# One work list for both layers of a two-layer encoder trunk: adding transfers, row sums and fillers placed elsewhere in the order

## The chip, the cores and the metric

The kernel runs on one core of one Trainium2 chip. The metric is device time in microseconds (us). Times of one kernel are medians of several runs; a profiled execution gives the trace on which the reading rests.

The engines are TensorE (PE, matmuls and transposes; its weight loads are listed as PEld), VectorE (DVE), ScalarE (ACT), GpSimd (POOL) and SyncE (SP). Each runs its own instructions in order, and they meet through semaphores. Transfers between the chip's main memory and the on-chip memory are issued by SP, ACT or POOL, and run on 16 DMA engines.

## The reference

Two layers run over a sequence of 512 rows of width 1024, in float32. Cut to its core, a layer is:

```python
h = x @ w_in[l]                     # 1024 x 9216, cut into eleven parts
o_a = retention(rq, rk, rv, rg)     # 4 heads, chunkwise recurrent form
o_b = chunk_attention(cq, ck, cv)   # 8 heads, relative bias, chunk-causal
o_c = diff_attention(dq, dk, dv)    # 4 heads, difference of two softmaxes
g = sigmoid(gates + b_merge[l])     # three gates per channel
merged = g0 * (o_a @ w_a) + g1 * (o_b @ w_b) + g2 * (o_c @ w_c)
x = layer_norm(ALPHA * x + merged @ w_out)
u_gate, u_up = split(x @ w_ffn_in)  # hidden width 2816
x = layer_norm(ALPHA * x + (silu(u_gate) * u_up) @ w_ffn_out)
```

## The kernel before

**Numbers.** Every float32 operand of a product is carried as a pair, a rounded high part and the rest as a low part, both in the format float32r. One product is three matmuls: high by high, high by low, low by high (`mm3`, lines 166 to 170). The pair is made by one cast on ACT (high) and one subtract on DVE (low). For activations this is `split` with `part_hi` and `part_lo` (lines 152 to 160); for weights it is line 203 and the one after it (plain tiles, class `Wt`, two halves each), and lines 310 and 311 (staged blocks, class `Staged`).

**Seven products in place of eight.** Most large products are done as 2 by 2 blocks by a scheme of Winograd's kind: seven block products, called m1, m2, y, x, g, v and h, on sums and differences of blocks. The sums of weights are made partly by DMA: the first block is loaded on SP (line 223), and a second is added to it on its way by a transfer that POOL issues with an add (line 227, `more`). Such a transfer is called an adding transfer here. Class `Adds` (input projections and FFN input) has two per problem: `a`, used by y, x and h, and `c`, used by g; where x and h need one more block, DVE adds it (line 307). Class `Chain` (FFN output) changes its block `a` in place: y is split, then an adding transfer turns `a` into what x needs, then, after x's split, a second turns it into what h needs (`take`, with `then`). m1, m2 and v are plain loads. The sums of activations are called row sums: for the input x they are made by `Quarters.turned` (lines 337 to 340 and two splits, s12 and s43), one call per pair of row blocks, named q0 to q3 in the list. The hidden rows of the FFN get theirs in class `Hidden` (steps h0.y, h0.m1 and so on; tiles hqh and hql).

**Memory.** Loaded weights lie in 4 buffers (`st`), split weights in 3 pairs of buffers (`wh`, `wl`), activations in 61 buffers of 128 by 512, and results of matmuls in 8 banks of PSUM. A block's load must wait until the split of an earlier block has freed its `st` buffer, and a split until PE has done with the block three before it.

**The order.** It is written out by hand in the string `ORDER` (lines 59 to 99). Entries are parted by `;`. The first word names an item, that is, one weight block and its matmuls: `w` (the values of attention b and c), `R` (queries and keys of the retention), `G1` (a gate), `p` and `q` (values and gates of the retention), `g20` and the like (plain gate tiles), `cqk` and `dqk` (queries and keys of the two attentions), `b01` (branch 0, tile 1), `out`, `ffn`, `i0` to `i3` (FFN input), `f18` to `f21` (plain FFN input tiles), `o0` and `o1` (FFN output) and `rest`. After it, parted by `|`, stand steps that are put between the item's jobs: after the first job, after the second, and so on. `+` splits the next block that isn't split yet (`prepare`). `w.a`, `w.c`, `o1.a` and so on issue the load and the adding transfer. `c1.3` to `c3.3` and `d0.30` to `d4.3` are the steps of the attentions: scores with softmax (c1, d0), transposes (c2, d2), products with the values (c3, d3) and the last transposes (d4). `rr`, `rf`, `rs` and `r1` to `r3` belong to the retention. Before each item, loads are issued until three blocks are ahead, and the item's own block is split if it is not yet (`run_items`).

The list gives each instruction its turn; the framework then lays out each engine's queue and may let an instruction of a later entry go ahead where it finds the engine free. In the string of before, the two layers have a list each, parted by `@`.

Of the kernel before, what the change touches and what calls it, by code (L numbers as in the profile page):

```python
# [55 lines left out]
NATURAL = ("m1", "m2", "y", "g")  # L56


ORDER = """first | q1 w.a ; w.m1 | + | + q2 q0 q3 ; w.m2 | lam | + w.c ; g03 ; w.y | + ; w.x |  | + ;
w.g | + + | R.a + ; w.v ; w.h | R.c + + | + ; R.m1 ; R.m2 |  | + ; R.y |  | + ; R.x | rr.000 | + ;  # L60
R.g | rr.010 | G1.a + ; R.v | + rr.101 ; R.h | rr.111 | G1.c ; G1.m1 | + rr.100 ; G1.m2 |  | + rr.110 ;
G1.y | rr.001 ; G1.x | rr.011 ; G1.g | + | rf.0 ; G1.v | dh.0 rs.0 | + ; p.m1 | p.a | r1.0 ;
G1.h | dh.1 | + ; p.m2 | p.c rf.1 | rs.1 + ; p.y |  | + ; p.x |  | + ; p.g | r1.1 q.a | + ; p.v |  | + ;
q.m1 | + | + ; p.h |  | r2.0 ; q.m2 | q.c + rf.2 r2.1 | + dh.2 ; q.y ; q.x | rs.2 | r3.1 ;
q.g | r3.0 rf.3 | + rs.3 dh.3 + ; q.v | r1.2 ; q.h | + r1.3 ; cqk1 | + + r2.3 r2.2 | r3.3 ; cqk0 | r3.2 ;
b01 | c1.0 | c1.1 vbc c2.0 + ; b02 | c1.2 + c3.0 c2.1 | c1.3 ; cqk2 |  | c3.1 c2.2 + + ;
b00 | c1.4 c3.2 | c2.3 c1.5 ; cqk3 | c3.3 + | c2.4 ; b03 | c1.6 + c3.4 c1.7 vbd + | c2.5 + ;
dqk0 | c3.5 c2.6 c2.7 | c3.6 ; dqk1 |  | d0.00 c3.7 ; b10 ; g20 | d0.01 + d0.10 | d2.0 ;
b13 | d3.0 + | + d0.11 ; dqk2 |  | + d2.1 ; b11 |  | d0.20 + d3.1 ; dqk3 | d0.21 d4.0 ; b12 | + | d2.2 + ;
g21 | + d0.30 | d3.2 d0.31 ; g23 | + | d2.3 ; g22 | d4.1 d4.2 d3.3 | + d4.3 ; b20 | + + ; b21 ; b22 |  | + ;  # L70
out0 ; b23 | + | + ; out1 ; out2 ; ffn | i0.a | i0.c + ; i0.m1 | n1 + | + n0 ; i0.m2 | + + ;
i0.y | + | + n2 ; i0.x ; i0.g |  | + i1.a n3 + ; i0.h ; i0.v ; i1.m1 | i1.c | + ; i1.m2 |  | + ; i1.y | + + ;
i1.x ; i1.g | i2.a | + ; i1.h |  | + + ; i1.v |  | + ; i2.m1 | i2.c + ; i2.m2 | + | + ; i2.y | + | + ; i2.x ;
i2.g |  | i3.a + ; i2.h |  | + ; i2.v | + ; i3.m1 ; i3.m2 | i3.c ; i3.y | + ; i3.x |  | + ;
i3.g |  | o0.a + ; i3.h |  | + o0.c o0.begin h0.y + ; i3.v |  | + ; f18 | + h0.m1 o0.rows ;
o0.m1 | h0.m2 | h0.x ; o0.y | + | h0.g ; o0.m2 | + + | h0.v ; f19 ; o0.x | h0.h | o1.begin + o1.a ;
o0.v |  | h1.y ; o0.g | + + | + ; o0.h | h1.m1 + o1.c | + ; o1.y | + h1.x + | h1.m2 ; o1.m1 ; o1.m2 ;
f20 | h1.v | + ; o1.x | h1.g h1.h + ; o1.g | + | + ; o1.v |  | + + ; f21 ; o1.h | + ; rest0 ; rest1 | + | + ;
rest2 ; @ ; first | + w.a q1 ; w.m1 |  | lam + q2 q0 q3 ; w.m2 |  | + ; g03 | w.c ; w.y | + ; w.x |  | + ;
w.g | + + | R.a + ; w.v ; w.h | R.c + + | + ; R.m1 ; R.m2 |  | + ; R.y |  | + ; R.x | rr.000 | + ;  # L80
R.g | rr.010 | G1.a + ; R.v | + rr.101 ; R.h | rr.111 | G1.c ; G1.m1 | + rr.100 ; G1.m2 |  | + rr.110 ;
G1.y | rr.001 ; G1.x | rr.011 ; G1.g | + | rf.0 ; G1.v | dh.0 rs.0 | + ; p.m1 | p.a | r1.0 ;
G1.h | dh.1 | + ; p.m2 | p.c rf.1 | rs.1 ; p.y |  | + + ; p.x |  | + ; p.g | r1.1 | + ; p.v | q.a | + ;
q.m1 | + | + ; p.h |  | r2.0 ; q.m2 | q.c + rf.2 r2.1 | + dh.2 ; q.y ; q.x | rs.2 | r3.1 r3.0 ;
q.g |  | rf.3 + + ; q.v | rs.3 dh.3 | r1.2 ; q.h | + | r1.3 + ; cqk1 | + r2.3 r2.2 | r3.3 ; cqk0 | r3.2 ;
b01 | c1.0 | c1.1 vbc c2.0 + ; b02 | c1.2 + c3.0 c2.1 | c1.3 ; cqk2 |  | c3.1 c2.2 + + ;
b00 | c1.4 c3.2 | c2.3 c1.5 ; cqk3 | c3.3 + | c2.4 ; b03 | c1.6 + c3.4 c1.7 vbd + | c2.5 ;
dqk0 | + c3.5 c2.6 c2.7 | c3.6 ; dqk1 |  | d0.00 c3.7 ; b10 ; g20 | d0.01 + d0.10 | d2.0 ;
b13 | d3.0 + | + d0.11 ; dqk2 |  | d2.1 + ; b11 |  | d0.20 + d3.1 ; dqk3 | d0.21 d4.0 ; b12 |  | d2.2 + ;
g21 | + d0.30 + | d3.2 d0.31 ; g23 | + | d2.3 ; g22 | d4.1 d4.2 d3.3 | + d4.3 ; b20 | + + ; b21 ;  # L90
b22 |  | + ; out0 ; b23 |  | + ; out1 | + ; out2 ; ffn | i0.a | i0.c + ; i0.m1 | n1 + | + n0 + ; i0.m2 | + ;
i0.y | + | + ; i0.x ; i0.g | n2 | + i1.a n3 + ; i0.h ; i0.v ; i1.m1 | i1.c | + ; i1.m2 |  | + ; i1.y | + + ;
i1.x ; i1.g | i2.a | + ; i1.h |  | + + ; i1.v |  | + ; i2.m1 | i2.c + ; i2.m2 | + | + ; i2.y | + | + ; i2.x ;
i2.g |  | i3.a + ; i2.h |  | + ; i2.v | + ; i3.m1 ; i3.m2 | i3.c | + ; i3.y ; i3.x |  | + ;
i3.g |  | o0.a + ; i3.h |  | + o0.c o0.begin h0.y + ; i3.v |  | + ; f18 | + h0.m1 o0.rows ;
o0.m1 | h0.m2 | h0.x ; o0.y | + | h0.g ; o0.m2 | + + | h0.v ; f19 ; o0.x | h0.h | o1.begin + o1.a ;
o0.v |  | h1.y ; o0.g | + + | + ; o0.h | h1.m1 + o1.c | + ; o1.y | + h1.x + | h1.m2 ; o1.m1 ; o1.m2 ;
f20 | h1.v | + ; o1.x | h1.g h1.h + ; o1.g | + | + ; o1.v |  | + + ; f21 ; o1.h | + ; rest0 ; rest1 | + | + ;
rest2"""


# [1 line left out]
def trunk(ctx, tc, x_in, xT_in, w_in, ret_norm_g, da_norm_g, lq1, lk1, lq2, lk2, w_a, w_b, w_c, b_merge, w_out,  # L103
# [463 lines left out]
    def item(specs, fn, *groups):  # L567

        items.append((specs, fn, groups))
# [75 lines left out]
    def layer(l):  # L645
# [933 lines left out]
        for i, it in enumerate(fout_rest(0) + fout_rest(1)):  # L1579
            its[f"rest{i}"] = it  # L1580
        fns["+"] = prepare
        for line in ORDER.split("@")[l].strip("; \n").split(";"):
            name, *groups = [part.split() for part in line.split("|")]
            item(*its[name[0]], *[[fns[n] for n in grp] for grp in groups])

# [8 lines left out]
    for l in range(LAYERS):  # L1594
        layer(l)
# [48 lines left out]
```

## Time and profile before

| | us |
|---|---|
| median of 3 runs | 1905.19 |
| lowest and highest run | 1901.96, 1908.35 |
| the profiled execution | 1906.96 |
| its span, from the first to the last instruction | 1905.2 |
| PE busy in the span | 1872.0 |
| DVE busy | 1393.9 |
| ACT busy | 1024.5 |
| mean granted clock of PE, as a share of full speed | 0.994 |

How to read it: a row of a timeline has the start, the duration, the engine, the line of the kernel, the operation, the output and the inputs, and in brackets how long the engine had been idle before, and who released it. A row of the waits has the waiting engine with its tile and line, whom it waited for, the total, the times and the longest. The granted clock is the share of TensorE's full clock in a stretch; at half of it a matmul takes about twice as long. Matmuls are pipelined, so the start-to-start distance of two of them is shorter than the duration of one.

### The profile page before, as it was taken

What the parts mean: (1) busy time and instruction counts of PE and PEld (TensorE: products, weight loads), DVE (VectorE), ACT (ScalarE), POOL (GpSimd) and SP (SyncE); (2) the same over time, 40 slices, a digit from 0 to 9 for tenths busy, and PEclk for the clock granted to TensorE, in tenths of its full rate; (3) what the DMA queues carried; (4) which work ended last, traced back from release to release, by engine and by line L of the source; (5) the groups of instructions that cost most, each with busy time, mean ns of one, the idle gap of its engine ahead of it and who ended that gap; (6) DMA issues with size and microseconds to landing.
All of it is one profiled execution on the core that took longest, in us unless ns stands there. A gap on an engine that the chain in (4) does not pass through costs nothing. (4 is left out here: it accounts for less than half of the span.)

```text
span 1905.2 us, 27735 instructions
## 1 busy us (share of the span) xinstructions
PE 1872.0 (98%) x10930; PEld 1655.2 (87%) x10930; DVE 1393.9 (73%) x2029; ACT 1024.5 (54%) x1651; POOL 116.8 (6%) x125
## 2 busy tenths in 40 slices
PE   9899999999999999999999999999999999999998
PEld 7799888887888999987898998888788889999876
DVE  4777876668757977786577878766686679777766
ACT  4556666677643644453265565576766345445431
POOL 0000100000001000010000001000000010000100
PEclk9999999999999999999999999999999999999999
DMA  8797755243256396876467896453332655769841
GB/s 278 219 271 228 194 177 160 67 149 111 78 171 188 96 241 164 234 190 165 144 191 232 230 255 193 149 172 101 109 118 94 204 133 160 183 180 252 208 134 45
DMA packets 233207, 327.29 MB, mean 172 GB/s; under 512 B 10751, under 2 KB 109173, under 8 KB 233077
## 3 DMA queue, kind: packets, MB, share of 16 engines
q1 hardware_dynamic: 197812, 260.50, 41.4%
q0 software_dynamic: 27456, 54.53, 16.4%
q10 hardware_dynamic: 7808, 10.49, 1.5%
q8 instruction: 86, 1.41, 0.3%
q14 instruction: 45, 0.36, 0.1%
HBM read 293.97 MB, written 31.51 MB: 171 GB/s over the span
## 5 line engine op out<-in xcount | busy, mean ns | idle before, releaser
L168 PE MATMUL pt<-xTh,wh 128*128 128x256 f32 (+1 forms) x1392 | 460.8, 332 | 0.9 <-ACT wh L203 0.9
L169 PE MATMUL pt<-xTl,wh 128*128 128x256 f32 (+1 forms) x1392 | 458.2, 329 | 1.3 <-DVE xTl L158 1.3
L170 PE MATMUL pt<-xTh,wl 128*128 128x256 f32 (+1 forms) x1392 | 458.1, 329 | 0.0
L311 DVE TENSOR_TENSOR wl<-st,wh 128x2048 fp32r<-128x2048 f32 x154 | 352.1, 2288 | 141.0 <-ACT wh L310 140.7
L310 ACT CAST wh<-st 128x2048 fp32r<-128x2048 f32 x154 | 293.5, 1910 | 277.6 <-PE pt L169 125.5
L169 PEld LDWEIGHTS pt<-xTl,wh 128*128 128x128 f32 x1392 | 265.6, 191 | 24.0 <-DVE xTl L158 1.8
L170 PEld LDWEIGHTS pt<-xTh,wl 128*128 128x128 f32 x1392 | 265.2, 191 | 23.8
L168 PEld LDWEIGHTS pt<-xTh,wh 128*128 128x128 f32 x1392 | 264.9, 191 | 23.9 <-ACT wh L203 1.6
L204 DVE TENSOR_TENSOR wl<-st,wh 128x1024 fp32r<-128x1024 f32 (+1 forms) x172 | 181.6, 1071 | 103.8 <-ACT wh L203 101.1
L203 ACT CAST wh<-st 128x1024 fp32r<-128x1024 f32 (+1 forms) x172 | 155.4, 928 | 168.5 <-issue 74.5
L168 PE MATMUL pt<-s43h,wh 128*128 128x256 f32 x384 | 109.1, 284 | 0.0
L169 PE MATMUL pt<-s12l,wh 128*128 128x256 f32 x384 | 108.9, 284 | 0.0
L170 PE MATMUL pt<-s12h,wl 128*128 128x256 f32 x384 | 108.9, 284 | 0.0
L168 PE MATMUL pt<-s12h,wh 128*128 128x256 f32 x384 | 108.9, 283 | 0.0
L169 PE MATMUL pt<-s43l,wh 128*128 128x256 f32 x384 | 108.8, 283 | 0.0
L170 PE MATMUL pt<-s43h,wl 128*128 128x256 f32 x384 | 108.8, 283 | 0.0
L168 PE MATMUL pf<-wh,hqh 128*128 128x512 f32 x224 | 89.9, 402 | 4.3 <-ACT hqh L154 4.3
L170 PE MATMUL pf<-wh,hql 128*128 128x512 f32 x224 | 90.0, 402 | 1.6 <-DVE hql L160 1.6
L169 PE MATMUL pf<-wl,hqh 128*128 128x512 f32 x224 | 89.2, 398 | 0.0
L307 DVE TENSOR_TENSOR st<-st 128x2048 f32<-128x2048 f32 x36 | 82.3, 2285 | 0.7 <-DMA st<-in_w_in 0.3
L168 PEld LDWEIGHTS pt<-s43h,wh 128*128 128x128 f32 x384 | 73.8, 192 | 0.2
L168 PEld LDWEIGHTS pt<-s12h,wh 128*128 128x128 f32 x384 | 73.8, 192 | 0.0
(306 smaller groups left out, 4008.5 us busy)
## 6 DMA issues: line engine op xcount, KB each, us to landing
st<-in_w_in SPq DMA_DIRECT2D x64, 1024.0 KB
st<-in_w_ffn_in SPq DMA_DIRECT2D x40, 1024.0 KB
st<-in_w_ffn_out SPq DMA_DIRECT2D x24, 1024.0 KB
st<-in_w_in POOLq DMA_DIRECT2D x20, 1024.0 KB, 10.1
st<-in_w_in SPq DMA_DIRECT2D x32, 512.0 KB
st<-in_w_ffn_in POOLq DMA_DIRECT2D x16, 1024.0 KB, 10.0
st<-in_w_ffn_out POOLq DMA_DIRECT2D x16, 1024.0 KB, 10.2
st<-in_w_ffn_in SPq DMA_DIRECT2D x24, 512.0 KB
```

The costliest lines, as they stand in the source:

```text
L168: nc.tensor.matmul(ps, lh, rh, start=start, stop=False, skip_group_check=more)
L169: nc.tensor.matmul(ps, lh, rl, start=False, stop=False, skip_group_check=more)
L170: nc.tensor.matmul(ps, ll, rh, start=False, stop=stop, skip_group_check=more)
L203: return [nc.scalar.copy(self.hi[:, a:b], self.st[:, a:b]), nc.vector.tensor_sub(self.lo[:, a:b], self.st[:, a:b], f(self.hi[:, a:b]))]
L204: nc.vector.tensor_sub(self.lo[:, a:b], self.st[:, a:b], f(self.hi[:, a:b]))]
L307: nc.vector.tensor_add(st, st, ap)
L310: nc.scalar.copy(self.hi, st)
L311: nc.vector.tensor_sub(self.lo, st, f(self.hi))
```

## The change

`ORDER` is replaced by one list that both layers use; the function that reads it takes the whole string for each layer instead of the part before or after `@`. The items, their matmuls, loads, splits and steps are the same; only their places differ.

In the first items of each layer (before, layer 0, then after):

```diff
-first | q1 w.a ; w.m1 | + | + q2 q0 q3 ; w.m2 | lam | + w.c ; g03 ; w.y | + ; w.x |  | + ;
+first | q1 + w.a | + q2 ; w.m1 |  | lam + q0 q3 ; w.m2 ; g03 | w.c + ; w.y |  | + ; w.x |  | + ;
```

Layer 1 had `first | + w.a q1 ; w.m1 |  | lam + q2 q0 q3 ; w.m2 |  | + ; g03 | w.c ; w.y | + ; w.x |  | + ;`.

In the attentions (before is layer 0; in layer 1 some `+` stood elsewhere):

```diff
-b01 | c1.0 | c1.1 vbc c2.0 + ; b02 | c1.2 + c3.0 c2.1 | c1.3 ; cqk2 |  | c3.1 c2.2 + + ;
+b02 | c1.0 | c1.1 vbc c2.0 + ; b01 | c1.2 + c3.0 c2.1 | c1.3 ; cqk2 |  | c3.1 c2.2 + ;
...
-dqk0 | c3.5 c2.6 c2.7 | c3.6 ; dqk1 |  | d0.00 c3.7 ; b10 ; g20 | d0.01 + d0.10 | d2.0 ;
-b13 | d3.0 + | + d0.11 ; dqk2 |  | + d2.1 ; b11 |  | d0.20 + d3.1 ; dqk3 | d0.21 d4.0 ; b12 | + | d2.2 + ;
-g21 | + d0.30 | d3.2 d0.31 ; g23 | + | d2.3 ; g22 | d4.1 d4.2 d3.3 | + d4.3 ; b20 | + + ; b21 ; b22 |  | + ;
+dqk0 | + c2.6 c2.7 c3.5 | c3.6 ; dqk1 |  | d0.00 c3.7 ; b10 ; g20 | d0.01 + + d0.10 | d2.0 ;
+b13 | d0.11 | d3.0 ; dqk2 | d2.1 + ; b12 | d3.1 | d0.20 + ; dqk3 | + d4.0 | d0.21 ; b11 | + | + ;
+g21 | d2.2 + | d0.30 d3.2 d0.31 ; g23 | + + | d2.3 ; g22 | d4.1 d4.2 d3.3 | d4.3 ; b20 | + ; b21 ;
```

In the FFN output (both layers):

```diff
-i3.g |  | o0.a + ; i3.h |  | + o0.c o0.begin h0.y + ; i3.v |  | + ; f18 | + h0.m1 o0.rows ;
-o0.m1 | h0.m2 | h0.x ; o0.y | + | h0.g ; o0.m2 | + + | h0.v ; f19 ; o0.x | h0.h | o1.begin + o1.a ;
-o0.v |  | h1.y ; o0.g | + + | + ; o0.h | h1.m1 + o1.c | + ; o1.y | + h1.x + | h1.m2 ; o1.m1 ; o1.m2 ;
-f20 | h1.v | + ; o1.x | h1.g h1.h + ; o1.g | + | + ; o1.v |  | + + ; f21 ; o1.h | + ; rest0 ; rest1 | + | + ;
+i3.g |  | o0.begin o0.a + ; i3.h |  | + o0.c o0.rows h0.y ; i3.v |  | h0.m1 + ; f18 ; o0.m1 |  | + ;
+o0.y | + | h0.x h0.m2 ; o0.m2 | h0.v | + + ; f19 | h0.h h0.g | + ; o0.x |  | o1.begin o1.a ; o0.g | + + ;
+o0.v | + | h1.y ; o0.h | h1.m1 + | + o1.c ; o1.m1 | + + | h1.m2 ; o1.y | h1.x ; o1.m2 |  | + ;
+f20 | h1.v | + ; o1.x | h1.h | h1.g ; o1.v | + + ; o1.g ; f21 |  | + ; o1.h | + ; rest0 ; rest1 | + + ;
```

Elsewhere the `+` stand at other places too; two more pairs of items change sides (`R.h` goes behind `G1.m1`, `i2.v` ahead of `i2.h`), some steps of the retention move by a job or two, and `p.a`, `q.a`, `q.c` and `i2.a` move by up to an item. The function:

```diff
-        for line in ORDER.split("@")[l].strip("; \n").split(";"):
+        for line in ORDER.split(";"):
```

More of the change, by code (lines that the diff above doesn't have):

```diff
@@ L56 @@
 NATURAL = ("m1", "m2", "y", "g")
[L59 to L63, printed above, removed]
@@ L64 @@
-q.m1 | + | + ; p.h |  | r2.0 ; q.m2 | q.c + rf.2 r2.1 | + dh.2 ; q.y ; q.x | rs.2 | r3.1 ;
-q.g | r3.0 rf.3 | + rs.3 dh.3 + ; q.v | r1.2 ; q.h | + r1.3 ; cqk1 | + + r2.3 r2.2 | r3.3 ; cqk0 | r3.2 ;
-b01 | c1.0 | c1.1 vbc c2.0 + ; b02 | c1.2 + c3.0 c2.1 | c1.3 ; cqk2 |  | c3.1 c2.2 + + ;
-b00 | c1.4 c3.2 | c2.3 c1.5 ; cqk3 | c3.3 + | c2.4 ; b03 | c1.6 + c3.4 c1.7 vbd + | c2.5 + ;
-dqk0 | c3.5 c2.6 c2.7 | c3.6 ; dqk1 |  | d0.00 c3.7 ; b10 ; g20 | d0.01 + d0.10 | d2.0 ;
-b13 | d3.0 + | + d0.11 ; dqk2 |  | + d2.1 ; b11 |  | d0.20 + d3.1 ; dqk3 | d0.21 d4.0 ; b12 | + | d2.2 + ;
@@ L70 @@
-g21 | + d0.30 | d3.2 d0.31 ; g23 | + | d2.3 ; g22 | d4.1 d4.2 d3.3 | + d4.3 ; b20 | + + ; b21 ; b22 |  | + ;
[L71 to L74, printed above, removed]
@@ L75 @@
-i3.g |  | o0.a + ; i3.h |  | + o0.c o0.begin h0.y + ; i3.v |  | + ; f18 | + h0.m1 o0.rows ;
-o0.m1 | h0.m2 | h0.x ; o0.y | + | h0.g ; o0.m2 | + + | h0.v ; f19 ; o0.x | h0.h | o1.begin + o1.a ;
-o0.v |  | h1.y ; o0.g | + + | + ; o0.h | h1.m1 + o1.c | + ; o1.y | + h1.x + | h1.m2 ; o1.m1 ; o1.m2 ;
-f20 | h1.v | + ; o1.x | h1.g h1.h + ; o1.g | + | + ; o1.v |  | + + ; f21 ; o1.h | + ; rest0 ; rest1 | + | + ;
-rest2 ; @ ; first | + w.a q1 ; w.m1 |  | lam + q2 q0 q3 ; w.m2 |  | + ; g03 | w.c ; w.y | + ; w.x |  | + ;
@@ L80 @@
[L80 to L95, printed above, removed]
@@ L96 @@
-o0.m1 | h0.m2 | h0.x ; o0.y | + | h0.g ; o0.m2 | + + | h0.v ; f19 ; o0.x | h0.h | o1.begin + o1.a ;
-o0.v |  | h1.y ; o0.g | + + | + ; o0.h | h1.m1 + o1.c | + ; o1.y | + h1.x + | h1.m2 ; o1.m1 ; o1.m2 ;
-f20 | h1.v | + ; o1.x | h1.g h1.h + ; o1.g | + | + ; o1.v |  | + + ; f21 ; o1.h | + ; rest0 ; rest1 | + | + ;
+ORDER = """first | q1 + w.a | + q2 ; w.m1 |  | lam + q0 q3 ; w.m2 ; g03 | w.c + ; w.y |  | + ; w.x |  | + ;
+w.g | R.a + | + + + ; w.v ; w.h | R.c + ; R.m1 | + + ; R.m2 | + ; R.y | + + ; R.x | rr.000 ;
@@ new lines @@
+R.g | rr.101 rr.010 | G1.a + ; R.v | + ; G1.m1 | + rr.100 ; R.h | rr.111 | G1.c ; G1.m2 |  | rr.110 ;
+G1.y | + | + rr.001 ; G1.x | rr.011 ; G1.g |  | + rf.0 ; G1.v | dh.0 rs.0 ; p.m1 |  | p.a r1.0 ;
+G1.h | dh.1 + | + ; p.m2 | p.c | rf.1 ; p.y ; p.x | + rs.1 | + ; p.g | + | r1.1 q.a ; p.v |  | + ;
+q.m1 | + | rf.2 ; p.h | + | r2.1 q.c ; q.m2 |  | + r2.0 + dh.2 ; q.y ; q.x | rs.2 | r3.1 r3.0 ;
+q.g | rf.3 | + rs.3 + dh.3 + ; q.v | r1.2 ; q.h | r1.3 | + ; cqk1 | + + r2.3 r2.2 | r3.3 ; cqk0 | r3.2 ;
@@ new lines @@
+b02 | c1.0 | c1.1 vbc c2.0 + ; b01 | c1.2 + c3.0 c2.1 | c1.3 ; cqk2 |  | c3.1 c2.2 + ;
+b00 | c1.4 c3.2 | c2.3 c1.5 ; cqk3 | c3.3 + | c2.4 + ; b03 | c1.6 + c3.4 c1.7 vbd | c2.5 ;
+dqk0 | + c2.6 c2.7 c3.5 | c3.6 ; dqk1 |  | d0.00 c3.7 ; b10 ; g20 | d0.01 + + d0.10 | d2.0 ;
+b13 | d0.11 | d3.0 ; dqk2 | d2.1 + ; b12 | d3.1 | d0.20 + ; dqk3 | + d4.0 | d0.21 ; b11 | + | + ;
+g21 | d2.2 + | d0.30 d3.2 d0.31 ; g23 | + + | d2.3 ; g22 | d4.1 d4.2 d3.3 | d4.3 ; b20 | + ; b21 ;
+b22 |  | + ; out0 ; b23 |  | + ; out1 ; out2 | + ; ffn | i0.a | + ; i0.m1 | n1 + | n0 ; i0.m2 | + i0.c + ;
@@ new lines @@
+i0.y | + | + n2 ; i0.x ; i0.g |  | + i1.a n3 + ; i0.h ; i0.v ; i1.m1 | i1.c | + ; i1.m2 |  | + + ; i1.y ;
+i1.x | + ; i1.g |  | + ; i1.h | i2.a | + + ; i1.v |  | + ; i2.m1 | i2.c + ; i2.m2 | + + | + ; i2.y | + ;
+i2.x ; i2.g |  | i3.a + ; i2.v ; i2.h | + ; i3.m1 ; i3.m2 | i3.c | + ; i3.y ; i3.x |  | + ;
+i3.g |  | o0.begin o0.a + ; i3.h |  | + o0.c o0.rows h0.y ; i3.v |  | h0.m1 + ; f18 ; o0.m1 |  | + ;
+o0.y | + | h0.x h0.m2 ; o0.m2 | h0.v | + + ; f19 | h0.h h0.g | + ; o0.x |  | o1.begin o1.a ; o0.g | + + ;
```

## The prediction

> **What bounds the kernel now.** I read the page's first part, then the waits of TensorE (PE), then stage windows around each wait, then each engine's timeline there.
>
> ```profile
> span 1905.2 us, 27735 instructions
> PE 1872.0 (98%) x10930; PEld 1655.2 (87%) x10930; DVE 1393.9 (73%) x2029; ACT 1024.5 (54%) x1651; POOL 116.8 (6%) x125
> ```
>
> PE is the bound: 33.2 us of the span are not busy. The change leaves every matmul in place, so it can win only what PE loses in waits, and what the clock loses around them. The waits of PE (total, times, longest):
>
> ```profile
> PE pf L168 <- ACT hqh L154: 4.3, 2, 2.3
> PE psc L442 <- ACT ks L152: 4.2, 2, 2.1
> PE pf L170 <- DVE s12l L158: 3.3, 2, 2.1
> PE pt L168 <- ACT obh L152: 3.0, 2, 1.5
> PE pf L168 <- ACT s12h L152: 2.1, 1, 2.1
> PE pf L170 <- DVE hql L160: 1.6, 2, 0.8
> PE psc L442 <- ACT th L1147: 1.1, 2, 0.5
> ```
>
> "2 times" is mostly once per layer. Three places hold most of it: the FFN output (hqh, hql), the row sums of x (s12, layer 0 only) and late attention (ks). The windows around them (PE, weight load, DVE, ACT, POOL busy, then granted clock, DMA share, GB/s), the FFN output and late attention in both layers:
>
> ```profile
> 63.00:79.00 16.00, 10.62 (x38) 7.61 (x37) 13.61 (x21) 7.54 (x11) 1.28 (x1) 0.89 0.45 159
> 471.00:476.00 5.00, 2.92 (x13) 2.28 (x12) 4.35 (x7) 4.18 (x6) 0.00 (x0) 0.85 0.24 87
> 866.00:878.00 12.00, 9.14 (x27) 6.74 (x26) 9.36 (x11) 5.58 (x6) 1.28 (x1) 0.72 0.53 167
> 1414.00:1419.00 5.00, 2.89 (x15) 2.19 (x14) 4.36 (x6) 3.83 (x6) 0.00 (x0) 1.00 0.38 139
> 1808.00:1820.00 12.00, 8.96 (x26) 6.52 (x25) 9.36 (x11) 5.58 (x6) 1.28 (x1) 0.72 0.50 156
> ```
>
> The loss at a place is its idle time plus (1 - clock) x window. FFN output: 4.3 + 1.6 idle, plus 12 x 0.28 = 3.4 in each layer, 12.7 together. Row sums: 3.3 + 2.1 = 5.4 idle, plus 16 x 0.11 = 1.8, so 7.2. Late attention: 4.2 idle, plus 5 x 0.15 = 0.8, so 5.0. **24.9 us in all.**
>
> **Part 1, the FFN output.** Each weight block is split by one ACT cast and one DVE subtract, whose groups on the page are
>
> ```profile
> L311 DVE TENSOR_TENSOR wl<-st,wh 128x2048 fp32r<-128x2048 f32 x154 | 352.1, 2288 | 141.0 <-ACT wh L310 140.7
> L310 ACT CAST wh<-st 128x2048 fp32r<-128x2048 f32 x154 | 293.5, 1910 | 277.6 <-PE pt L169 125.5
> ```
>
> Timelines of PE, ACT, DVE, SP and POOL in layer 0, and the adding transfers' line of the page:
>
> ```profile
> 866.12 0.39 PE L168 MATMUL pf<-wh,hqh 128*128 128x512 f32 x1
> 867.25 0.39 PE L170 MATMUL pf<-wh,hql 128*128 128x512 f32 x1
> 869.71 0.50 PE L168 MATMUL pf<-wh,hqh 128*128 128x512 f32 x1 [2.07 <-ACT hqh L154]
> 867.14 1.99 ACT L203 CAST wh<-st 128x1024 fp32r<-128x1024 f32 x2 [8.16 <-DMA st<-in_w_ffn_in]
> 869.03 0.62 ACT L154 ACTIVATE hqh<-fth 128x512 fp32r<-128x512 f32 x1
> 851.96 2.29 DVE L311 TENSOR_TENSOR wl<-st,wh 128x2048 fp32r<-128x2048 f32 x1
> 854.27 1.97 SPq L196 DMA_DIRECT2D st<-in_w_ffn_in  x2
> 849.25 1.28 POOL L227 DMA_DIRECT2D st<-in_w_ffn_out  x1 [24.48 <-DVE wl L311]
> 850.95 1.28 POOL L227 DMA_DIRECT2D st<-in_w_ffn_out  x1 [0.42 <-issue]
> st<-in_w_ffn_out POOLq DMA_DIRECT2D x16, 1024.0 KB, 10.2
> ```
>
> ACT works in order. The casts of the plain tile f20 (L203) stood 8.16 us for its load; behind them stood the second half of h1.m2's cast (hqh), which PE wanted at 867.5 for o1.m2, after six matmuls of it (866.12 to 867.25 are five steps, 0.227 each). The load was issued at 854.27, when the split of o1.m1 (wl, 851.96 + 2.29) freed its st buffer, and took 12.9 us, because two adding transfers of about 10.2 us each had begun at 849.25 (o1.y's, behind y's split) and 850.95 (o1.c's).
>
> The new list puts o1.m1 ahead of o1.y, one item of 24 matmuls (5.4 us of PE) earlier. What moves: m1's split (ACT cast, DVE subtract) starts 5.4 earlier, so SP issues f20's loads near 848.9; y's split and the adding transfer that POOL issues behind it move 5.4 later, to 854.6. f20's load then shares the engines with o1.c's addition alone. If it takes between 6.3 (1.05 MB at the 167 GB/s of the window 866:878) and the old 12.9, it lands between 855 and 861.8; its casts need a wh buffer, which PE frees at the end of o1.m1, one item and six matmuls before 867.5, at 860.7. So ACT waits at most 1.1, and h1.m2's half, 0.62 of cast, is ready by 865. The casts cost nothing then; the cover is PE's item between. The y transfer, now at 854.6 + 10.2 = 865, meets o1.x's cast, which is wanted only after o1.m2's end (871.6) and f20's 48 matmuls (10.9), at 882: hidden. The x, g, v, h order likewise frees o0.c before v; no wait of PE stood there. I take **12.7** (bounds 0 and 12.7).
>
> On the clock there is a rule to weigh: the window's clock is 0.72 after waits of 2.1 and 0.8 us, but 1.00 after a wait of 2.1 at 1415. The Trainium skill, "TensorE: Matmul & The Clock Gate", section "What's actually happening", has the clock halve after an idle window of about 3.4 us; by that no wait here would slow the clock, and only idle time would come back. The trace disagrees at 866, agrees at 1414; I follow the windows, and keep the other as rival D.
>
> **Part 2, row sums of x.**
>
> ```profile
> 63.11 0.39 PE L168 MATMUL pf<-wh,s12h 128*128 128x512 f32 x1
> 74.00 0.50 PE L170 MATMUL pf<-wh,s12l 128*128 128x512 f32 x1 [2.13 <-DVE s12l L158]
> 40.10 0.42 DVE L337 TENSOR_TENSOR sa<-xf 128x256 f32<-128x256 f32 x1
> 50.24 1.23 DVE L204 TENSOR_TENSOR wl<-st,wh 128x1024 fp32r<-128x1024 f32 x1 [9.04 <-ACT wh L203]
> 61.91 2.29 DVE L307 TENSOR_TENSOR st<-st 128x2048 f32<-128x2048 f32 x1 [0.29 <-DMA st<-in_w_in]
> 64.72 2.28 DVE L307 TENSOR_TENSOR st<-st 128x2048 f32<-128x2048 f32 x1
> 73.26 0.68 DVE L158 TENSOR_TENSOR s12l<-sa,s12h 128x512 fp32r<-128x512 f32 x1
> 37.52 0.37 SPq L223 DMA_DIRECT2D st<-in_w_in  x1
> 53.01 20.73 SPq L223 DMA_DIRECT2D st<-in_w_in  x3
> ```
>
> w.y wants the sums q0 to q3 from 63.1 on; the last half came at 73.9. DVE had stood 9.04 us at g03's split, with q1's fourth operation behind it, and between the late sums ran two additions for w.x and w.h (L307, 4.6) and two splits (4.6): 9.2 us of work not yet wanted. The new list puts q1 and q2 ahead of g03's split and q0, q3 right behind it, and w.x's split behind all of w.y. A sum is four quarter operations (0.42) and two differences (0.68), about 3 us of DVE; two of the four now fit the 9.04 us gap, and 9.2 of foreign work lies lower. The last half was wanted nine matmuls into w.y, at 65.1, and came 8.8 late: the second alone covers that, and the first adds 6. That is 7.2 won.
>
> A price goes with it. Buffers of loads are handed out in list order: before, w.c's load took the one freed at 37.5 and w.x's the one at 53.0; now w.x's load is issued first (three blocks ahead, at g03), so w.c's goes out near 53. It landed then in 8.9 (53.01 to 61.9), POOL adds 1.28 and 10.2, ACT's cast 1.9: 75.3, and the subtract 2.3 more. PE reaches w.g at 63.1 + 2 x 5.4 = 73.9: a wait of 1.4 to 3.7, or about nothing if the load takes 6.3. I take 2. Behind that cast stand ACT's copies of w.x's result (tu), which only later sums want. Part 2: **5.2** (bounds -3.7 and 7.2). Layer 1 had no such wait; it loses and gains nothing.
>
> **Part 3, late attention.**
>
> ```profile
> 473.99 0.99 PE L442 MATMUL psc<-ks,qs 128*128 128x512 f32 x4 [2.08 <-ACT ks L152]
> 466.88 1.08 ACT L152 CAST dPh<-ptr 128x512 fp32r<-128x512 f32 x2
> 468.25 2.35 ACT L404 COPY sw<-pt 32x512 f32<-32x512 f32 x4
> 472.68 2.54 ACT L152 CAST ks<-rot 64x512 fp32r<-64x512 f32 x4
> L1109 PE MATMUL pdo<-vhl,dPh 128*128 128x256 f32 x64 | 18.2, 346 | 0.0
> ```
>
> d0.20's scores (psc) wait for dqk2's key: its rotary copies begin behind d2.1's casts (1.1 us). The new list runs d2.1 between dqk2's two projections, so these casts leave the key's path, and d3.1 goes ahead of d0.20: 8 matmuls of this form and 2 like them, 0.346 each when alone, about 0.12 when packed (256 columns, half of 0.227), so 1.2 to 3.5 us of filler. Together 2.3 to 4.6 against 2.08: the wait goes, in both layers. d2.1 itself needs d0.11, which moves ahead of d3.0, so its input is not later. The obh wait (3.0) and the th wait (1.1) keep their neighbours (d0.00, c3.7, then b10; d0.01, d0.10 in g20): no change. I take **5.0** (bounds 0 and 9.1).
>
> **The rest of the list** (both layers now share one; splits mostly listed nearer their use; R.h one place later; loads p.a, w.a behind others; first of layer 1 fetched at rest1's end instead of in o1.h) I cannot read item by item. The cover of these moves is that PE waits nowhere else for long; the obh and th waits, 4.1 us, are the kind that stays over in such a list, and a new order can make as many again. I take -3 (bounds -6 and +4.1).
>
> **Sum:** 12.7 + 5.2 + 5.0 - 3 = 19.9. The profiled execution took 1906.96 in all (span 1905.2), 1.8 above the median of 1905.19. From the one 1887.1, from the other 1885.3: **1886 us**, 1% less.
>
> **Rivals.** **A, the load stays late** (chance 0.13): f20's split is still listed before h1.m2's cast, and the addition of o1.c still meets f20's load. If ACT again stands, part 1 gives nothing: 1886 + 12.7 = 1899. For it: the ACT order; against it: a load 5.4 us earlier with one addition less. **B, a new wait for the old one** (0.12): w.g's wait takes 3.7 and, with the clock, some 2 more, and small waits take 6: 1886 + 7 = 1893. **C, slower** (0.11): the splits. Their place in the list is nearer to use: counting the list, 84 of the 227 splits are listed one item or less ahead, 59 before. A split takes 1.9 + 2.3 = 4.2 against an item of 5.4: 1.2 us of slack, which one sum or rotary ahead of it takes. If the 25 newly late ones lose 2 us each, 50 us go: 1886 + 50 = 1936. It decides from 0.8 us each (20 in all), where the gain is gone. Against it: ACT's casts mostly wait for PE to free a wh buffer (125.5), not for their turn, so the list's place does not set their start. **D, the clock does not come back** (0.05): if the slow stretches of 3.4 + 3.4 + 1.8 + 0.8 = 9.4 are not caused by the waits, 1895. The skill's rule named above would have it so. **The forecast as it stands**: 0.59.
>
> **How the numbers follow.** About 0.3%, 5.7 us, is what a measurement can tell from no change: from 1899.5 to 1910.9 is "same". The forecast, B and D are faster (0.76), A lies on the border and goes mostly to same; C is slower. Faster 0.76, same 0.13, slower 0.11. Range: down to 1877 (all 24.9, and the 4 that the rest may win), up over A to 1904, which leaves out C and little else.
>
> **What would show it.** Right: no PE wait on hqh, s12 or ks; in the FFN output f20's L196 loads before y's L227; windows there at clock 1.00. Wrong: ACT's L203 waiting for st<-in_w_ffn_in near 860; PE waiting at w.g (pf, s43) for wh; new rows "PE <- ACT wh" or "PE <- DVE wl" summing to more than 6; then the splits are the bound.

## The result, and the profile after

| | median, us | lowest to highest | runs |
|---|---|---|---|
| before | 1904.01 | 1901.96 to 1908.35 | 4 |
| after | 1889.19 | 1888.39 to 1890.41 | 4 |

The ratio is 0.992 (95% interval 0.9901 to 0.9939), that is 15 us less. Line numbers of the changed kernel are 20 lower than before: L168 is now L148, L311 is L291, L223 is L203.

The head of the changed kernel's page, and then its waits of PE (who waits for whom: total us, times, longest). Left out are two rows that both kernels share (warm 1.5, xTl 1.3) and those of 0.5 and less:

```profile
span 1887.4 us, 27746 instructions
PE 1864.0 (99%) x10930; PEld 1648.8 (87%) x10930; DVE 1394.0 (74%) x2029; ACT 1022.9 (54%) x1651; POOL 116.3 (6%) x125
```

```profile
PE pf L150 <- DVE s12l L138: 2.7, 2, 1.7
PE pf L148 <- ACT s12h L132: 2.2, 2, 1.1
PE psc L422 <- ACT th L1127: 2.1, 2, 1.1
PE pro L149 <- DVE rvl L138: 1.5, 2, 0.7
PE pt L148 <- ACT obh L132: 1.1, 2, 0.6
PE pt L148 <- DVE do L1096: 0.9, 2, 0.5
```

The rows for hqh, hql and ks are gone. Those for s12 are not: 4.9 us, where before had 5.4. The windows of the changed kernel (PE, weight load, DVE, ACT, POOL busy, then clock, DMA share, GB/s), at the row sums, at late attention, and at the FFN output of both layers:

```profile
61.50:77.50 16.00, 11.17 (x40) 7.85 (x39) 14.50 (x24) 7.62 (x13) 0.83 (x1) 0.89 0.71 176
462.00:478.00 16.00, 15.55 (x81) 13.26 (x80) 10.21 (x19) 12.01 (x27) 0.00 (x0) 1.00 0.25 83
860.00:872.00 12.00, 12.00 (x55) 9.93 (x54) 9.55 (x11) 4.57 (x4) 1.28 (x1) 1.00 0.86 223
1793.00:1805.00 12.00, 12.00 (x55) 9.93 (x54) 9.46 (x12) 5.72 (x5) 1.28 (x1) 1.00 0.82 216
```

The FFN output now runs without a gap at full clock in both layers. At the row sums PE still stands idle, and the clock is still 0.89. Timelines of SP, POOL and ACT in the changed kernel, at the FFN output of layer 0:

```profile
845.60 0.99 SPq L176 DMA_DIRECT2D st<-in_w_ffn_in  x2
845.81 1.28 POOL L207 DMA_DIRECT2D st<-in_w_ffn_out  x1 [22.17 <-DVE wl L291]
851.30 1.28 POOL L207 DMA_DIRECT2D st<-in_w_ffn_out  x1 [4.21 <-DVE wl L291]
857.69 2.00 ACT L183 CAST wh<-st 128x1024 fp32r<-128x1024 f32 x2 [2.52 <-issue]
```

f20's loads go out ahead of the second adding transfer, and its casts no longer wait for them (8.16 us before). At the row sums of layer 0, the timelines of ACT, SP, DVE and POOL in the changed kernel:

```profile
48.63 0.33 ACTq L1140 DMA_DIRECT2D th<-th  x1
49.06 1.05 ACT L183 CAST wh<-st 128x1024 fp32r<-128x1024 f32 x1 [6.22 <-DMA rows<-in_ln_g]
67.40 1.90 ACT L290 CAST wh<-st 128x2048 fp32r<-128x2048 f32 x1 [3.71 <-DMA st<-in_w_in]
69.21 0.61 ACT L132 CAST s12h<-sa 128x512 fp32r<-128x512 f32 x1
39.80 0.27 SPq L651 DMA_DIRECT2D rows<-in_ln_g  x1
50.14 1.23 DVE L184 TENSOR_TENSOR wl<-st,wh 128x1024 fp32r<-128x1024 f32 x1 [7.90 <-ACT wh L183]
58.28 2.28 DVE L287 TENSOR_TENSOR st<-st 128x2048 f32<-128x2048 f32 x1
58.66 1.28 POOL L207 DMA_DIRECT2D st<-in_w_in  x1 [22.09 <-DVE s12l L138]
```

Read backwards: DVE still stands 7.90 us for ACT's cast of g03. ACT stands because the issue of its own store of a gate tile (th) waits 6 us, by the trace for a small load (rows) that SP issued at 39.80. The kernel before had the same stall, in two pieces (5.85 us here, 1.93 just ahead of g03's cast):

```profile
46.54 0.69 ACT L1147 ACTIVATE th<-pt,hb 128x512 f32<-128x512 f32 x1 [5.85 <-DMA rows<-in_b_merge]
```

From 50.14 until the last row sum is ready, near 74, DVE runs without a gap, so whatever stands in its queue ahead of a row sum delays it. Later ACT stands 3.71 us for w.g's block, whose addition POOL issued at 58.66, and the cast of the last row sum (69.21) is behind it. That second stall costs this sum only about 0.5 us, since DVE had made its input (sa) at 68.72 and no sooner.

### The profile page after: what moved, and what is told of

Read it like the earlier page. It is cut to its first block, busy times and chain, and to the rows that moved or that the text cites. A ratio compares the mean times of both kernels' runs of the same rounds, so it can differ in the third digit from the quotient of the medians.

```text
span 1887.4 us, 27746 instructions
## 1 busy us (share of the span) xinstructions
PE 1864.0 (99%) x10930; PEld 1648.8 (87%) x10930; DVE 1394.0 (74%) x2029; ACT 1022.9 (54%) x1651; POOL 116.3 (6%) x125
## 5 line engine op out<-in xcount | busy, mean ns | idle before, releaser
L148 PE MATMUL pt<-xTh,wh 128*128 128x256 f32 (+1 forms) x1392 | 460.0, 331 | 1.2 <-DVE do L1096 0.9
L291 DVE TENSOR_TENSOR wl<-st,wh 128x2048 fp32r<-128x2048 f32 x154 | 352.5, 2290 | 137.5 <-ACT wh L290 134.7
L148 PEld LDWEIGHTS pt<-xTh,wh 128*128 128x128 f32 x1392 | 264.3, 190 | 24.6 <-DVE do L1096 1.2
L148 PE MATMUL pt<-s43h,wh 128*128 128x256 f32 x384 | 109.1, 284 | 0.1
L148 PE MATMUL pt<-s12h,wh 128*128 128x256 f32 x384 | 108.7, 283 | 0.0
L148 PE MATMUL pf<-wh,hqh 128*128 128x512 f32 x224 | 87.3, 390 | 0.0
L287 DVE TENSOR_TENSOR st<-st 128x2048 f32<-128x2048 f32 x36 | 82.3, 2287 | 0.3
L148 PEld LDWEIGHTS pt<-s43h,wh 128*128 128x128 f32 x384 | 73.7, 192 | 0.7 <-DVE tw L838 0.6
L148 PEld LDWEIGHTS pt<-s12h,wh 128*128 128x128 f32 x384 | 73.7, 192 | 0.0
```

The source lines that it names most:

```text
L148: nc.tensor.matmul(ps, lh, rh, start=start, stop=False, skip_group_check=more)
L287: nc.vector.tensor_add(st, st, ap)
L291: nc.vector.tensor_sub(self.lo, st, f(self.hi))
```

## The experiments

All times are compared with the kernel before, run on the same chip beside them (medians 1905.10, 1903.99 and 1904.23 us for the three groups of four). "Split step" is a `+` of the list.

| run | median (lowest to highest), us | ratio (95% interval) |
|---|---|---|
| e1 FFN output alone | 1895.84 (1890.46 to 1898.27) | 0.995 (0.993 to 0.9969) |
| e2 late attention alone | 1898.24 (1894.58 to 1901.40) | 0.9963 (0.995 to 0.9976) |
| e3 row sums alone | 1917.82 (1913.96 to 1922.24) | 1.0069 (1.005 to 1.0089) |
| e4 one exchange alone | 1893.60 (1893.19 to 1897.09) | 0.9945 (0.9927 to 0.9962) |
| e5 after, small loads late | 1889.53 (1883.91 to 1895.43) | 0.9921 (0.9899 to 0.9942) |
| e6 before, small loads late | 1903.60 (1897.80 to 1907.49) | 0.9987 (0.9971 to 1.0002) |
| e7 row sums alone, same lead | 1903.42 (1900.84 to 1905.92) | 0.9997 (0.9987 to 1.0007) |
| e8 after, exchange undone | 1890.15 (1888.21 to 1892.55) | 0.9923 (0.9907 to 0.994) |
| e9 after, w.c earlier | 1896.45 (1893.27 to 1899.75) | 0.9953 (0.9938 to 0.9969) |
| e10 after, small loads late and w.c earlier | 1892.50 (1890.05 to 1900.88) | 0.9945 (0.9925 to 0.9964) |
| e11 after, FFN output of before | 1899.24 (1897.01 to 1901.42) | 0.9974 (0.9963 to 0.9984) |
| e12 after, once more | 1888.60 (1887.26 to 1891.85) | 0.9919 (0.9904 to 0.9935) |

### The parts, each alone in the list of before (e1, e2, e3)

Each takes one of the blocks of the diff as shown and leaves the rest of the two lists: e1 from `i3.g` to `rest1`, e2 from `b13` to `g21`, e3 from `first` to `w.x`.

> The sequence of before with the new order of the FFN output alone, in both layers. If the three parts are independent, as the forecast's sum has it, the new order gives its whole term: 12.7 us, ratio 0.993, the waits for hqh and hql gone and the clock of that stretch 1.00, while the waits for s12h, s12l and ks stand as before (about 11 us and 4 us). Rival: the gain hangs on where the rest of the list has left the engines by then; the waits stay above 4 us per layer and the ratio is over 0.996.

> The sequence of before with the new late attention alone, in both layers. By the forecast's third step: the two waits for ks (2.1 us each, and the clock behind them) go, 5.0 us, ratio 0.997, and the waits for th and obh stay at 1.1 and 3.0. If the order of the other parts had a hand in what the changed kernel shows, new small waits (do 0.9, th 1.0) come here too and the gain is 3 to 4 us, ratio 0.998.

> The sequence of before with the spread row sums alone, in both layers. The forecast's second step gives 5 to 7 us, ratio 0.997, with the waits for s12h and s12l below 1 us. The theory from the changed kernel's trace: ScalarE is held by a store whose issue waits and VectorE still has the split of g03, two splits and two additions ahead of the last row sum, so 4 to 5 us of waits for s12h and s12l stay, and the time is that of before within 1.5 us, ratio 0.999 to 1.000.

In us, by ratio times 1904: e1 won 9.5, e2 won 7.0, and e3 lost 13.1. In e1 and e2 the waits named went. The lead, that is, how many blocks ahead of its item a block is split, follows from the lists by counting. e2 changes it only inside its own block. e1 holds two split steps fewer, so its lead is one or two blocks less from i3.v to layer 1's G1.x, and its 9.5 us are not of the FFN output alone (a wait for rqkh in layer 0's retention is 1.9 us there, in the profile of before 0.6). The loss of e3 fits neither of its two expectations; most of it is in layer 1, far behind the edit, at the retention's rotated keys. One row of the waits of PE in e3, then its timelines there (SP, POOL, ACT):

```profile
PE psr L168 <- ACT rqkh L154: 9.4, 3, 6.4
```

```profile
1116.88 0.37 SPq L223 DMA_DIRECT2D st<-in_w_in  x1
1117.34 2.14 SPq L796 DMA_DIRECT2D rqr<-rqk  x2
1111.64 1.29 POOL L227 DMA_DIRECT2D st<-in_w_in  x1 [24.06 <-DMA st<-in_w_in]
1130.45 0.62 ACT L152 CAST rqkh<-rqr 128x512 fp32r<-128x512 f32 x1 [7.06 <-DMA rqr<-rqk]
```

Two reloads of 256 KB, issued from 1117.34 behind a plain weight load (1116.88) and an adding transfer (1111.64), landed only near 1130.4, and ACT stood 7.06 us for them. But why so late there? The new first items hold six split steps where the old ones held five. In layer 0 the sixth changes little: the old list had no lead at w.m1, and a block without lead is split at its own item anyway, so from w.y on the lead is that of before. In layer 1 the old list had lead in hand, so there the splits run one block further ahead than before from w.m1 to p.m1 (but for g03). The reload (rf.0, listed at G1.g) and PE's wait of 6.4 us (r1.0, at p.m1) lie inside that stretch.

### The same with the lead kept (e7)

```diff
-w.g | + + | R.a + ;
+w.g | + | R.a + ;
```

> The spread row sums alone, as in the run that was 12.7 us slower, but with one split step fewer at w.g, so that all later splits keep their lead over the list of before. If that run's new waits (rqkh, 9.4 us and the clock behind them) came from the splits of the rest standing one block earlier, they are gone here and the time is that of before within 1.5 us, ratio 0.9995 to 1.0005. If they came from the new places in the first items, the ratio is 1.005 or more again.

The loss is gone: 0.9997. In layer 1 the lead is that of before from w.v on (in layer 0 it is now one less from w.v to G1.y). So e3's 13 us were the price of one split step too many, not of the new places of the row sums, and the spread row sums themselves are worth nothing that can be measured. In the profile of e7 PE waits 3.7 us for s12h and 1.7 for s12l, as much as before.

### The exchange at the FFN output, done alone and undone alone (e4, e8)

```diff
-o1.y | + h1.x + | h1.m2 ; o1.m1 ; o1.m2 ;
+o1.m1 | + h1.x + | h1.m2 ; o1.y ; o1.m2 ;
```

> The sequence of before with one exchange in each layer: the plain tile o1.m1 is listed ahead of the adding tile o1.y, and nothing else moves. By the forecast's first step the load of f20 is then issued about 849 instead of 854.3 us and lands before its cast is due, and this alone gives 11 to 12.7 us, ratio 0.9935, with no wait for hqh and hql. Rival: the exchange is not enough, because another adding transfer still overlaps the load or the h1.m2 casts are listed too near; then waits of 2 us or more per layer stay, clock loss behind them, and the ratio is 0.996 to 0.998.

Two items exchanged per layer give 10.5 us. Timelines of e4 (SP, POOL, ACT):

```profile
848.87 0.99 SPq L196 DMA_DIRECT2D st<-in_w_ffn_in  x2
851.21 1.28 POOL L227 DMA_DIRECT2D st<-in_w_ffn_out  x1 [26.39 <-DVE z L1412]
860.97 2.00 ACT L203 CAST wh<-st 128x1024 fp32r<-128x1024 f32 x2 [1.96 <-issue]
```

f20's loads go out at 848.87, as forecast, ahead of both adding transfers (the other goes out at 854.58), ACT doesn't wait for them, and no wait for hqh or hql is left. The reverse, in the changed kernel:

```diff
-o1.m1 | + + | h1.m2 ; o1.y | h1.x ;
+o1.y | + + | h1.m2 ; o1.m1 | h1.x ;
```

> The changed kernel with one exchange undone in each layer: the adding tile o1.y ahead of the plain tile o1.m1 again. If the overlap of f20's load with o1.y's two adding transfers is the whole cause, the waits for hqh and hql come back (3 us per layer and the clock behind them) and most of the 12.7 us is lost: 1898 to 1902 us, ratio 0.997 to 0.9985. Rival: the other moves of the new list (splits listed nearer, h1.m2 first) cover it too; then less than 4 us is lost, ratio 0.992 to 0.994.

Nothing is lost (0.9923), though the stall itself is back. Timelines of e8 (SP, POOL, ACT, PE):

```profile
849.61 2.34 SPq L176 DMA_DIRECT2D st<-in_w_ffn_in  x2
844.37 2.59 POOL L207 DMA_DIRECT2D st<-in_w_ffn_out  x2 [22.20 <-DVE wl L291]
861.79 2.00 ACT L183 CAST wh<-st 128x1024 fp32r<-128x1024 f32 x2 [8.05 <-DMA st<-in_w_ffn_in]
863.70 0.62 ACT L134 ACTIVATE hqh<-fth 128x512 fp32r<-128x512 f32 x1
866.68 0.39 PE L150 MATMUL pf<-wh,hql 128*128 128x512 f32 x1
866.91 0.39 PE L148 MATMUL pt<-xTh,wh 128*128 128x512 f32 x1
```

ACT stands 8.05 us for the same load behind the same two adding transfers, and PE goes from o1.m2 (866.68) into f20 (866.91) without a gap. So a stalled ACT costs by what stands behind it. Before, that was the second half of h1.m2, which PE wanted at once. The new list names h1.m2 ahead of h1.x, so by the list the cast left behind the stall (863.70) is one of h1.x's, and o1.x comes only behind f20. That this order is the second cure is read from the list and these rows and isn't shown; it wasn't tried by itself.

### The FFN output of before in the changed kernel, and the changed kernel again (e11, e12)

e11 puts the old lines from `i3.g` on into the new list, with a `+` more at `i3.x` and three fewer at `o1.h` and `rest1`.

> The changed kernel with the order of the FFN output of before in both layers (one split step more ahead of it and three fewer at its end, so that the lead there is that of before). If the term of 12.7 us stands for itself, it is lost here: the waits for hqh and hql are 5 to 6 us again with the clock behind them, 1900 to 1903 us, ratio 0.998 to 0.9995. If the other parts of the new list had already covered the late load, the ratio stays below 0.995.

> The changed kernel once more, beside the others on the same chip, as the measure for the two edits at the row sums: 1889 us, ratio 0.992, with waits for s12h and s12l between 3 and 5 us in the profiled execution.

The changed kernel repeats its ratio. Its waits for s12h and s12l are 5.1 us here, and the clock from 61.5 to 77.5 is 1.00 where its first profile had 0.89. The difference of the two ratios, e11's and e12's, is 0.0055, 10.5 us. In e11 the waits are back (hqh 4.2, hql 1.2), but part of the clock is not: see the windows below. Not all of the 10.5 need be the FFN output: e11's profile also has a wait of 2.7 us for rqkh in layer 0's retention, where its list is still that of the changed kernel, which has no such wait in either profile.

### What holds the row sums (e5, e6, e9, e10)

e5 and e6 keep the seven small loads of layer 1's vectors out of layer 0's start; the order on PE, DVE and ACT stays the same.

```diff
-            nc.gpsimd.memset(rows, 0.0)
+            (tc.keep_in_program_order if l else lambda i: i)(nc.gpsimd.memset(rows, 0.0))
```

> The changed kernel with one edit: the seven small loads of layer 1's vectors (rows), which it issues at 36.6 to 50 us, stand at the end of layer 0 instead; nothing else moves. Theory 1: what kept the row sums late is ScalarE, whose store of a gate tile waited from 42.8 to 48.6 us for such a load (5.85 to 6.2 us in both kernels), so that the cast and split of g03, and behind them the second half of every row sum, came 6 us late. Then the split starts near 44 us, the waits for s12h and s12l (4.9 us) fall below 1.5 us, the clock of 61.5 to 77.5 us is 0.97 or more, and the time is 5 to 6.5 us below the changed kernel: 1883 to 1885 us, ratio 0.989. Theory 2: the two splits and two additions of other blocks that stand ahead of the last row sum on VectorE are what counts; then the waits at 61.8 and 63.6 us go and those at 68.4 and 72.1 us (1.1 and 1.7 us) stay, and the gain is 2 to 3 us, ratio 0.991. If the store only waits for another transfer, nothing is won: 0.992.

> The same edit in the kernel before, with its row sums where they were. Theory 1 has the list's new places of the row sums for nothing: the waits for s12h and s12l (5.4 us) fall below 1.5 us here too, 5 to 7 us, ratio 0.9965. Theory 2: the waits at 66.8 and 71.5 us stay (2.1 us each), gain 1 to 2 us, ratio 0.999.

Timelines of e5 (ACT, DVE, POOL, PE):

```profile
43.63 1.05 ACT L183 CAST wh<-st 128x1024 fp32r<-128x1024 f32 x1 [0.45 <-ACT th L1127]
44.71 1.22 DVE L184 TENSOR_TENSOR wl<-st,wh 128x1024 fp32r<-128x1024 f32 x1 [2.14 <-ACT wh L183]
55.69 1.29 POOL L207 DMA_DIRECT2D st<-in_w_in  x1 [19.00 <-DMA st<-in_w_in]
64.73 1.90 ACT L290 CAST wh<-st 128x2048 fp32r<-128x2048 f32 x1 [4.74 <-DMA st<-in_w_in]
66.53 0.61 ACT L132 CAST s12h<-sa 128x512 fp32r<-128x512 f32 x1
67.20 0.50 PE L148 MATMUL pf<-wh,s12h 128*128 128x512 f32 x1 [2.93 <-ACT s12h L132]
```

The first half of theory 1 holds: without the small loads ACT isn't held, and g03's split runs at 44.71, 5.4 us earlier than after. The clock from 61.5 to 77.5 is 1.00 here, as theory 1 had it. The second half fails: PE still waits 2.93 us for s12h, and 0.6 for s12l. About half of the 2.93 is ACT's 4.74 us for w.g's block, whose addition went out at 55.69: DVE had made the sum's input (sa) at 65.01, and the cast ran at 66.53. The other half is DVE's own queue, which runs without a gap from 51.76. So theory 2, the work ahead of the sums on DVE, keeps a part. The median, 0.9921, is that of the changed kernel. e6, at 0.9987, can't be told from no change, though its waits for s12h and s12l are 3.4 us where before had 5.4. e9 and e10 then move that addition forward:

```diff
-w.m2 ; g03 | w.c + ;
+w.m2 |  | w.c ; g03 | + ;
```

> The changed kernel with one step moved: the load of w.g's block and its adding transfer (w.c) are issued at w.m2, ahead of the load for w.x, in place of g03. In the changed kernel ScalarE's cast for w.g stood 3.7 us for that adding transfer, issued at 58.7 us, ahead of the last row sum's cast. Theory: this alone moves the stall to the load for w.x, which then comes after g03's split (52.9 us) and lands near 60 us, so the waits for s12h and s12l stay at 3 to 5 us and the time is that of the changed kernel within 1.5 us, ratio 0.992. Rival: the adding transfer is what counts, and 2.5 us or more are won, ratio below 0.991.

> The changed kernel with both edits: the seven small loads at the end of layer 0, and w.c issued at w.m2. Theory: the two together take away what ScalarE stands for ahead of the row sums (6.2 us for the small load, 3.7 to 4.7 us for w.g's block); no wait for s12h or s12l above 0.7 us is left, the clock of 61.5 to 77.5 us is 1.00, and the time is 4.5 to 6.5 us below the changed kernel on the same chip, ratio 0.989. Rival: VectorE's two splits and two additions still stand ahead of the last row sum and keep 2 us or more of waits; then the gain is under 3 us.

Both are slower than the changed kernel: e9 by 0.0034 of the ratio (6.5 us, with intervals apart), e10 by 0.0026 (5 us, its interval overlaps that of e12 a little). Timelines of e10 (SP, POOL, DVE, PE):

```profile
36.34 11.87 SPq L203 DMA_DIRECT2D st<-in_w_in  x2
47.81 1.29 POOL L207 DMA_DIRECT2D st<-in_w_in  x1 [10.82 <-DVE wl L184]
60.61 2.29 DVE L287 TENSOR_TENSOR st<-st 128x2048 f32<-128x2048 f32 x1 [5.91 <-DMA st<-in_w_in]
65.56 0.79 PE L148 MATMUL pf<-wh,s12h 128*128 128x512 f32 x1 [4.06 <-ACT s12h L132]
```

Now w.x's load (the second of SP's two, issued near 47.8) runs beside w.c's addition (47.81) and lands only when DVE starts its addition, at 60.6, some 12.7 us later; in e5 a load issued at the same time, with no adding transfer issued beside it, had landed by 55.69, some 8 us later. DVE stands 5.91 us, with the rest of the row sums behind it in order. It is f20's story once more: a plain load beside an adding transfer came late. None of these orders is faster than the changed kernel.

## Why the prediction was right, and where it was not

The forecast was 1886 us with 1877 to 1904 as its range, and 1889.2 was measured. Its likeliest case came true in the whole and in two of three parts; the third failed, and two sizes were off. Of the 19.9 us forecast, 14.8 were won. That the total is only 5 short is in part luck: the row sums gave nothing of their 5.2, and the misses of the other terms (about -2 to -3, +2 and +1) nearly cancel.

**Part 1, FFN output: right in event and place, its size probably too large by about 2.** The forecast named f20's load, its earlier issue and the clock, and the profile after shows them. The size was 12.7; the runs give 9.5 (e1), 10.5 (e4) and 10.5 (e12 less e11). Each of these has an interval of 3 to 4 us to each side, which still holds 12.7, so the size is judged from windows, not from medians. The idle term of 5.9 holds (5.4 in e11). The term that was mis-sized is the clock, "12 x 0.28 in each layer", read from one execution. The same place in other kernels with the same waits, window by window for layer 0 and layer 1 (PE busy, then clock; all engines in e2 and e3, PE alone in e11):

```profile
863.00:875.00 12.00, 9.47 (x41) 7.22 (x40) 9.84 (x12) 7.50 (x7) 1.28 (x1) 1.00 0.56 174
1801.00:1813.00 12.00, 8.87 (x26) 6.42 (x25) 9.54 (x12) 5.71 (x7) 1.28 (x1) 0.72 0.49 150
```

```profile
867.00:879.00 12.00, 9.58 (x29) 6.97 (x28) 10.05 (x12) 6.55 (x7) 1.28 (x1) 0.72 0.56 158
1825.00:1837.00 12.00, 8.82 (x32) 6.51 (x31) 9.96 (x12) 7.20 (x7) 1.28 (x1) 0.86 0.50 146
```

```profile
866.00:878.00 12.00, 9.55 (x34) 0.86 0.54 138
1804.00:1816.00 12.00, 9.08 (x33) 0.86 0.49 145
```

The clock of the 12 us is 1.00, 0.86 or 0.72, that is a loss of 0, 1.7 or 3.4 us. With the two of before, these eight windows lose 18.5 us (3.4 four times, 1.7 three times, and nothing once), 2.3 each, so 4.6 for the two layers in place of 6.7; with 5.9 of idle time that makes 10.5, where the medians of the runs lie. e6 and e7 have the same waits; their clocks there are 0.72 and 0.86, and 0.86 twice, and with them the twelve windows lose 2.2 each. The forecast had taken the largest of the three steps twice. And e8 shows that the load's earlier issue, which the forecast made its whole cause, was enough (e4) but not needed.

**Part 2, row sums: failed.** The step was "two of the four now fit the 9.04 us gap, and 9.2 of foreign work lies lower". In the profile after the gap is still 7.90 with q1's fourth operation behind it, and both additions (L287) still run ahead of the last row sum: the framework gave DVE almost the old order. Forecast 5.2, measured nothing (e7). The forecast had asked whom DVE waited for (ACT) and not whom ACT waited for; the small load was in the trace of before. It is no full answer either: with it gone (e5) the waits for s12 fall from 4.9 to 3.5 us only, behind the next late block and DVE's own queue. The price for w.c was put in the wrong place. No wait of PE at w.g came; ACT's wait for that block (3.7) stood ahead of the row sum's cast instead, at a cost of about 0.5. And w.c's late place pays, since an early one is 6.5 us worse (e9).

**Part 3, late attention: right.** Forecast 5.0, measured 7.0 (4.6 to 9.5) in e2, and no wait for ks is left. The clock term, 5 x 0.15 = 0.8, was read in a window that is too short for its slow stretch: from 462 to 478 the kernel before has 0.89, which is 1.8, and that makes 6.0. That obh and th would not change was wrong for the whole list (3.0 to 1.1, and 1.1 to 2.1), and a wait for do (0.9) is new. In e2 obh stays at 3.0 and th at 1.1 while do is there, so the changes of obh and th come from outside e2's block; from where wasn't tried.

**The rest: -3.** The parts alone win 9.5 + 0.6 + 7.0 = 17.1, the whole 15.2: 1.9 lost, by difference only, and the intervals of the three are 2 to 4 us to each side. It fits the -3, and isn't shown.

**The rivals.** A (the load stays late) didn't come; e8 shows that it would have cost nothing in the new list. B didn't come at w.g, where PE has no wait; its small waits came in part (th 1.0 more, rvl 1.5 and do 0.9 new, against 1.9 less for obh). C has its mechanism in e3, with the sign turned: the 13 us came from splits one step too early, not too late, and most of it at a reload of the retention that the forecast had not looked at. D didn't come: at the FFN output the clock comes back where the waits go, in both layers.

What stays open: an order in which both w.x's load and w.c's addition land in time, or in which DVE's queue holds less ahead of the sums, and how much of the 4.9 us it would return; and the spread of e5's times (1883.9 to 1895.4), wider than that of the changed kernel.

## What to carry to other kernels

When a wait ends on an engine that was itself standing, ask for that engine's own last wait, and for what stands behind it in order: removing one link hands the time to the next, and a long stall costs nothing if only late work is behind it. Keep adding transfers away from a plain load that is due soon; beside one a load took 12.7 us here (e10), without one some 8 (e5). When one part of a hand-written order is tried alone, keep the lead of everything behind it, or the trial measures the lead. A clock loss read from one execution is one draw: look at the same stretch in several.

## What the runs showed of the hardware

**The clock falls in steps.** In the twelve windows above, two waits of 1.6 to 3.0 and of 0.4 to 0.8 us, with two matmuls between them, left a clock of 1.00, 0.86 or 0.72 over the 12 us: none, one or two stretches of about 3.4 us at half speed (half of 3.4 is 1.7, which is 0.14 of 12). The length of the waits alone doesn't decide. Timelines of PE in e2, and then in e3:

```profile
866.65 0.50 PE L168 MATMUL pf<-wh,hqh 128*128 128x512 f32 x1 [1.74 <-ACT hqh L154]
868.17 0.50 PE L170 MATMUL pf<-wh,hql 128*128 128x512 f32 x1 [0.79 <-DVE hql L160]
```

```profile
869.61 0.50 PE L168 MATMUL pf<-wh,hqh 128*128 128x512 f32 x1 [1.63 <-ACT hqh L154]
871.14 0.79 PE L170 MATMUL pf<-wh,hql 128*128 128x512 f32 x1 [0.79 <-DVE hql L160]
```

The longer pair left the next matmul at 0.50 us, the shorter one at 0.79. The Trainium skill, "TensorE: Matmul & The Clock Gate", section "What's actually happening", has a window of about 3.4 us that runs freely, whatever the kernel does; the steps agree with it. That it takes a whole idle window does not agree: 1.63 and 0.79 us of idle time were enough.

**A small load can hold an engine for 6 us.** ACT's store at 48.63 waited, by the trace, for a load of 4 KB that SP had issued at 39.80 behind 1 MB of weights; without those small loads (e5) the 6.22 us before g03's cast fell to 0.45. Why a store waits for another queue's load the trace does not say.
